# Gates of the middle group added by indirect transfers into cleared arrays, in place of one-hot products

## The chip, the cores and the metric

The kernel runs on one core of a Trainium2 chip. The metric is the device time of one execution in microseconds; the number compared is the median of three runs. Engines are named as in the profile: PE (TensorE), DVE (VectorE), ACT (ScalarE), POOL (GpSimd) and SP (SyncE, which issues most transfers).

## What is computed

One decoder layer over 1024 tokens of width 1024: a mixer (latent attention and retention, merged by gates) and then a channel mixer of single-neuron experts. The change touches the second:

```python
q = (x @ w_peer_q).reshape(T, 8, 128)            # 8 heads
s1, s2 = q[..., :64] . keys_1, q[..., 64:] . keys_2   # 128 keys each
v1, i1 = top_k(s1, 16); v2, i2 = top_k(s2, 16)
sc, ci = top_k(v1[:, None] + v2[None, :], 16)    # 16 pairs per head
eidx = e1 * 128 + e2                             # one of 16384 experts
gates = softmax(sc)                              # 8 x 16 gates per token
act = gelu(x . peer_u[eidx])
y = sum_k gates_k * act_k * peer_v[eidx_k]
```

So each token has 128 (expert, gate) pairs, and the same expert may come from two heads, whose gates add.

## The kernel before

The 1024 tokens are 8 blocks of 128, in three groups: blocks 0 to 2, 3 and 4, 5 to 7 (`GROUPS`, line 29). For each group the mixer runs in order: `latents` (projections to queries and keys), `mix` (retention and attention, interleaved), `merge`, `output` (projection, norm, top-k scores). `interleave` (line 284) weaves two generators by the counts in `STEPS`. The weights come in pieces of 512 KB through a ring of three `raw` tiles; each piece is split by ACT into a high part `whi` and by DVE into a rest `wlo` (`split_piece`, line 220), and every product is three matmuls (`mm3`).

Side work runs from two queues, `background[0]` and `background[1]`. `pace` (line 165) gives each queue a credit for each weight piece, by the rates in `RATES`; a queue's generators run while they have credit, each step costing what it yields. So how many side steps run is set by pieces, not by time.

The experts are done in two ways. For blocks 0 to 2 the rows of `peer_u` and `peer_v` are gathered: `gathered` (line 1059, in `background[1]`) fetches one row per token with an indirect transfer from POOL (line 1064, 512 KB), four rows ahead, and DVE takes one dot product (line 1081) or one weighted addition (line 1090) per step; 256 steps a block, 1.2 of credit each. For blocks 3 to 7 all 16384 experts are computed densely, in `dense` (line 1130). There a key e is one value of e2, with 128 experts: `scores(e)` (line 1152) multiplies one piece of `peer_u` with the 640 tokens. The first 48 keys (`AHEAD`) are computed in a first stage and stored in `gl_d`; then, in the last stage, groups of 8 keys are multiplied by their gates (`weights`, line 1213) and with `peer_v`, summed in PSUM, and added to y.

The gates of the dense blocks form a matrix of 128 x 128 experts by tokens. `gate_matrix` (line 1097) makes it from one-hot products: for 8 tokens DVE compares the two key indices with a ramp (line 1120), ACT copies one result, DVE multiplies the other by the gates (line 1123), PE multiplies the two for each token (line 1108), ACT copies the product out (line 1110), and after 32 tokens SP stores 2 MB to `gate_d` (line 1113). That is 16 steps per block, 80 in all, run from `background[0]` during the first dense stage. In the last stage `gate_tile` (line 1202) loads the gates of four keys in rows of 512 bytes.

For blocks 3 and 4 the pairs are chosen (`choose`, line 982) while the last group's mixer runs; what comes out is kept in `routed` until the dense stage. The start of `dense` loads these blocks' tokens back from `xT_d` (line 1144).

Of the kernel before, what the change touches and what calls it, by code (L numbers as in the profile page):

```python
# [12 lines left out]
F32 = mybir.dt.float32  # L13
# [10 lines left out]
P = 128  # L24
# [4 lines left out]
GROUPS = ((0, 1, 2), (3, 4), (5, 6, 7))  # L29
NGROUP = 1  # L30
NGATH = sum(len(g) for g in GROUPS[:NGROUP])
ND = NBLK - NGATH
# [15 lines left out]
DELAY = 8.0  # L48
STEPS = (((86, 72), (116, 64), (116, 144)), ((112, 90), (112, 90), (112,)), (80, 50))
HEAD = 20  # L50
# [44 lines left out]
def layout(inputs):  # L95
# [34 lines left out]
    col = lambda v: np.ascontiguousarray(v.reshape(-1, P).T)  # L130
    o["g_cols"] = np.concatenate([col(a["g_ret_gn"][0]), col(a["g_q_lora"][0]), col(a["g_kv_lora"][0])], 1)
    o["g_mix"] = a["g_mix"]
# [12 lines left out]
def hybrid_layer(ctx: ExitStack, tc: tile.TileContext, out, a, dbg=None):  # L145
# [48 lines left out]
    def bcast(ap, n, off=0):  # L194
# [8 lines left out]
            for g, blocks in enumerate(GROUPS[NGROUP:-1])]  # L203
    gate_d = dram.tile([DT // TS, P, P * TS], F32, name="gate_d")
    gl_d = dram.tile([AHEAD, P, DT], F32, name="gl_d")
# [98 lines left out]
    routed = []  # L304
    routing = []


# [7 lines left out]
    def group(g):  # L315
# [273 lines left out]
        def retention(hp):  # L589
# [5 lines left out]
            if meta:  # L595
                nc.sync.dma_start(tab[:, nbk], tb[:, NBLK])
            qk = rp.tile([P, nb, 4, 2, 32], F32, name="qk")
            tb2 = rp.tile([P, nb, 4, 2, 32], F32, name="yn")
# [191 lines left out]
        def open_mix():  # L790
            finish(0, LEAVE[0][g])
            own.mps, mp = pool("mp")
            own.oT = [mp.tile([P, W], F32, name=f"oT{k}") for k in range(4)]
            own.yT = [mp.tile([P, W], F32, name=f"yT{k}") for k in range(KD)]
            own.rps, own.rp = pool("rp")
            own.qb = own.rp.tile([P, nbk, 2, P], F32, name="qbd")
            V.memset(own.qb, 0.0)
            own.retentions = chain(*(retention(hp) for hp in range(4)))

        def mix():  # L800
            start(1)
            aps, own.ap = pool("ap")
            interleave([own.retentions, attention()], STEPS[0][g])
            aps.close()
            own.rps.close()

# [39 lines left out]
        def output():  # L846
# [20 lines left out]
            if not last:  # L867
                if g >= NGROUP:
                    ktp = ctx.enter_context(tc.tile_pool(name=f"kt{g}", bufs=1, side="right", reuse_waits="tile"))
                fcs, fc = pool("fc", "right")  # L870
                scs = [pool(f"sc{i}_", "right") for i in reversed(range(nbk))][::-1]
            xps, xp = pool("xp", "right")
            xT = [xp.tile([P, KD, W], F32R, name=n) for n in ("xT_hi", "xT_lo")]
# [57 lines left out]
            def route_pairs(i):  # L931
                found = yield from choose(blocks[i], *top[i], fc, ktp)
                if ktp:
                    routed.append(found)
                else:
                    background[1].append(gathered(blocks[i], *found))
# [45 lines left out]
    def choose(b, tv, ti, fp, ktp=None):  # L982
# [61 lines left out]
        if not ktp:  # L1044
            eidx = work.tile([P, 128], I32, name="eidx", bufs=NGATH)
            V.scalar_tensor_tensor(eidx, e12[:, 0], 128.0, e12[:, 1], op0=OP.mult, op1=OP.add)
            return eidx, gate
        pt = zacc()[:, 0]
        for s in range(2):
# [9 lines left out]
    def gathered(b, eidx, gate):  # L1059
# [16 lines left out]
        for n in range(256):  # L1076
# [5 lines left out]
            else:  # L1082
# [14 lines left out]
    def gate_matrix(i, kt, gT, iota_2, p):  # L1097

        stage = {}

        def products(t8, pairs):
# [10 lines left out]
            if t8 == t0 + TS - 8:  # L1112
                nc.sync.dma_start(gate_d[(P * i + t0) // TS], stage[0].rearrange("p e t -> p (e t)"))

        pending = None
        for t8 in range(0, P, 8):
            at = lambda t: t.rearrange("p (q r) -> p q r", r=2).unsqueeze(2).to_broadcast([P, 4, P, 2])
            eq = [p.tile([P, 4, P, 2], BF16, name=f"eq{n}", bufs=2) for n in range(2)]
            for n in range(2):
                V.tensor_tensor(eq[n], iota_2.unsqueeze(1).to_broadcast([P, 4, P, 2]), at(kt[:, n, t8:t8 + 8]), OP.is_equal)  # L1120
            pairs = [p.tile([P, 4, P, 2], F32, name=n, bufs=2) for n in ("oa", "ob")]
# [8 lines left out]
    def dense(xT):  # L1130
        nt = DT // TS
        pacing["rates"] = RATES[3]
        last = GROUPS[-1]
        segments = [(xT, len(last) * P)]
        xdp = ctx.enter_context(tc.tile_pool(name="xd", bufs=1, side="right", reuse_waits="tile"))
        for g, blocks in enumerate(GROUPS[NGROUP:-1]):
            w = P * len(blocks)
            t = [xdp.tile([P, KD, w], F32R, name=f"x_{n}{g}") for n in ("hi", "lo")]
            per = 1024 // w
            for dst, src in zip(t, xT_d[g]):  # L1140
                for j in range(0, KD, per):
                    n = min(per, KD - j)
                    raw = wp.tile([P, 1024], F32, name="raw", bufs=RING)
                    nc.sync.dma_start(raw[:, :n * w].rearrange("p (j c) -> p j c", j=n), src[:, j:j + n])
                    S.activation(dst[:, j:j + n].rearrange("p j c -> p (j c)"), raw[:, :n * w], AF.Copy)
            segments.insert(g, (t, w))
# [3 lines left out]
        up = ups.enter_context(tc.tile_pool(name="up", bufs=1, reuse_waits="tile"))  # L1150

        def scores(e):
# [11 lines left out]
        def routes():  # L1164
# [16 lines left out]
            for i, (kt, gT) in enumerate(routed):  # L1181
                yield from gate_matrix(i, kt, gT, iota_2, gm)
            gms.close()
# [16 lines left out]
        gts = deque()  # L1200
# [25 lines left out]


        es = [4 * n + k for n in sorted(range(P // 4), key=lambda n: (n + 0.5) / AHEAD if 4 * n < AHEAD else
                                        (n + 0.5 - AHEAD / 4) / (P - AHEAD)) for k in range(4)]
        gate_tile(es[0])  # L1230
        for e0 in range(0, P, GE):
# [35 lines left out]
    ident = load_const("ident", a["c_ident"], [P, P])  # L1267
    g_cols = load_const("g_cols", a["g_cols"], [P, 13])
    g_gn, g_ql, g_kvl = g_cols[:, 0:8], g_cols[:, 8:11], g_cols[:, 11:13]
    g_gnh = const.tile([P, 8], F32, name="g_gnh")  # L1270
# [58 lines left out]
```

## Time and profile before

| | us |
|---|---|
| median of three runs | 3496.61 (3493.37 to 3500.15) |
| profiled execution | 3493.31 |
| its span, first to last instruction | 3491.5 |
| TensorE busy (matmul) | 3291.3 (94%) |
| VectorE busy | 2611.3 (75%) |
| ScalarE busy | 1261.8 (36%) |
| GpSimd busy | 1159.7 (33%) |
| mean busy share of the 16 DMA engines, 837 MB | 240 GB/s |

The stages, by the first and last instructions of their lines: group 0 to about 540 us, group 1 to 980, group 2 to 1420, first dense stage to 1955, last stage to 3490. A busy share over the whole span mixes these; for a change in one stage the rows of that stage count. Matmuls overlap in the pipeline, so durations of single ones add to more than the busy time.

### The profile page before, as it was taken

What the parts mean: (1) busy time and instruction counts of PE and PEld (TensorE: products, weight loads), DVE (VectorE), ACT (ScalarE), POOL (GpSimd) and SP (SyncE); (2) the same over time, 40 slices, a digit from 0 to 9 for tenths busy, and PEclk for the clock granted to TensorE, in tenths of its full rate; (3) what the DMA queues carried; (4) which work ended last, traced back from release to release, by engine and by line L of the source; (5) the groups of instructions that cost most, each with busy time, mean ns of one, the idle gap of its engine ahead of it and who ended that gap; (6) DMA issues with size and microseconds to landing.
All of it is one profiled execution on the core that took longest, in us unless ns stands there. A gap on an engine that the chain in (4) does not pass through costs nothing.

```text
span 3491.5 us, 53120 instructions
## 1 busy us (share of the span) xinstructions
PE 3291.3 (94%) x20376; PEld 3003.2 (86%) x20376; DVE 2611.3 (75%) x5118; ACT 1261.8 (36%) x2097; POOL 1159.7 (33%) x821
## 2 busy tenths in 40 slices
PE   8899989989789999899999899999999999999999
PEld 7788988788767799799999887888898888888888
DVE  4434458987697577689898687888888878878885
ACT  3445344544345533324666322222222222222221
POOL 0100000122211122012454354554556545555452
PEclk9999999999899999899999999999999999999999
DMA  3422354456744458446877998988989898989895
GB/s 132 124 78 85 123 188 135 151 179 235 255 148 142 136 200 297 160 156 209 309 285 286 338 314 285 326 317 310 321 305 345 300 328 309 334 304 318 308 333 182
DMA packets 329247, 837.10 MB, mean 240 GB/s; under 512 B 45712, under 2 KB 140688, under 8 KB 326176
## 3 DMA queue, kind: packets, MB, share of 16 engines
q1 hardware_dynamic: 218400, 431.00, 35.9%
q0 software_dynamic: 110592, 402.70, 32.8%
q8 instruction: 160, 2.62, 0.3%
q14 instruction: 95, 0.78, 0.1%
HBM read 755.16 MB, written 78.43 MB: 239 GB/s over the span
## 4 chain that ended last, share of the span: by engine, by line
PE 36%; issue 24%; POOL 11%; DVE 8%; DMA 5%; ACT 2%; POOLq 0%; SPq 0%; DVEq 0%; ACTq 0%
POOL row L1064 10%; PE zacc L245 7%; PE zacc L247 7%; PE zacc L246 7%; PE tr L245 3%; PE tr L246 3%; PE tr L247 3%; DMA row<-in_peer_v_dram,eidx 2%; PE tr L764 2%; DVE wlo L218 2%; DMA gl<-gl_d 1%; PE sc L728 1%; DVE row L1081 1%; PE sc L774 1%; DVE top_i L975 1%
## 5 line engine op out<-in xcount | busy, mean ns | idle before, releaser
L217 ACT ACTIVATE whi<-raw 128x1024 fp32r<-128x1024 f32 (+2 forms) x508 | 520.5, 1026 | 1337.5 <-PE zacc L247 619.7
L218 DVE TENSOR_TENSOR wlo<-raw,whi 128x1024 fp32r<-128x1024 f32 (+2 forms) x508 | 600.1, 1183 | 434.0 <-ACT whi L217 433.1
L1064 POOL DMA_INDIRECT row<-in_peer_u_dram,eidx x384 | 490.2, 1277 | 1004.1 <-DVE row L1081 791.3
L1064 POOL DMA_INDIRECT row<-in_peer_v_dram,eidx x384 | 602.7, 1570 | 610.8 <-DVE acc L1090 259.4
L245 PE MATMUL zacc<-whi,c_hi 128*128 128x512 f32 x1280 | 506.4, 396 | 39.1 <-DVE y L1254 37.6
L247 PE MATMUL zacc<-whi,c_lo 128*128 128x512 f32 x1280 | 504.5, 394 | 5.1 <-DVE c_lo L218 5.1
L246 PE MATMUL zacc<-wlo,c_hi 128*128 128x512 f32 x1280 | 504.1, 394 | 0.0
L1081 DVE SCALAR_TENSOR_TENSOR row<-row,xn 128x1024 f32<-128x1024 f32 x384 | 462.5, 1221 | 37.5 <-DMA row<-in_peer_u_dram,eidx 26.4
L245 PE MATMUL tr<-xT_hi,whi 128*128 128x384 f32 (+1 forms) x1216 | 410.8, 338 | 17.3 <-ACT gl L1161 16.2
L246 PE MATMUL tr<-xT_lo,whi 128*128 128x384 f32 (+1 forms) x1216 | 407.9, 335 | 0.0
L247 PE MATMUL tr<-xT_hi,wlo 128*128 128x384 f32 (+1 forms) x1216 | 407.5, 335 | 0.0
L245 PEld LDWEIGHTS zacc<-whi,c_hi 128*128 128x128 f32 x1280 | 244.3, 191 | 94.1 <-issue 36.4
L245 PE MATMUL tr<-x_hi,whi 128*128 128x256 f32 x1024 | 294.1, 287 | 9.6 <-ACT whi L217 9.6
L247 PEld LDWEIGHTS zacc<-whi,c_lo 128*128 128x128 f32 x1280 | 244.0, 191 | 58.9 <-DVE c_lo L218 7.2
L246 PE MATMUL tr<-x_lo,whi 128*128 128x256 f32 x1024 | 288.7, 282 | 0.0
L247 PE MATMUL tr<-x_hi,wlo 128*128 128x256 f32 x1024 | 288.6, 282 | 0.0
L246 PEld LDWEIGHTS zacc<-wlo,c_hi 128*128 128x128 f32 x1280 | 244.5, 191 | 50.3
L1090 DVE SCALAR_TENSOR_TENSOR acc<-row,dots,acc 128x1024 f32<-128x1024 f32 x192 | 246.0, 1281 | 18.3 <-DMA row<-in_peer_v_dram,eidx 17.8
L245 PE MATMUL zacc<-whi,hn_hi 128*128 128x256 f32 x832 | 250.7, 301 | 1.8 <-ACT pT L779 1.3
L1090 DVE SCALAR_TENSOR_TENSOR xn<-row,dots,xn 128x1024 f32<-128x1024 f32 x189 | 241.9, 1280 | 9.1 <-DMA row<-in_peer_v_dram,eidx 8.9
L245 PEld LDWEIGHTS tr<-xT_hi,whi 128*128 128x128 f32 x1216 | 231.3, 190 | 19.0 <-ACT gl L1161 16.8
L246 PE MATMUL zacc<-wlo,hn_hi 128*128 128x256 f32 x832 | 238.3, 286 | 0.9 <-DVE wlo L218 0.9
(268 smaller groups left out, 6929.5 us busy)
## 6 DMA issues: line engine op xcount, KB each, us to landing
raw<-in_peer_ut_dram SPq DMA_DIRECT2D x128, 512.0 KB, 5.4
raw<-in_peer_vt_dram SPq DMA_DIRECT2D x128, 512.0 KB, 6.6
gate_d<-stage SPq DMA_DIRECT2D x20, 2048.0 KB, 8.4
gt<-gate_d SPq DMA_DIRECT2D x32, 1280.0 KB, 9.8
raw<-in_w_nat_dram SPq DMA_DIRECT2D x72, 512.0 KB, 3.5
raw<-in_w_z_dram SPq DMA_DIRECT2D x48, 512.0 KB, 3.7
gl_d<-gl SPq DMA_DIRECT2D x48, 320.0 KB, 4.4
gl<-gl_d SPq DMA_DIRECT2D x48, 320.0 KB, 8.0
```

Of the source, the lines that this page charges most:

```text
L217: S.activation(hi, src, AF.Copy)
L218: V.tensor_tensor(lo, src, hi.bitcast(F32), OP.subtract)
L245: T.matmul(o, st[0], mv[0], start=first, stop=False)
L246: T.matmul(o, st[0], mv[1], start=False, stop=False)
L247: T.matmul(o, st[1], mv[0], start=False, stop=last)
L728: T.matmul(sc[:, c, 0:w], qh, kT[0:96, k0:k0 + w], start=True, stop=c < nch - 1)
L764: T.matmul(oo, vh[:, c + k], pT[:, k], start=False, stop=c + k == b)
L774: T.transpose(pt[:, P * k:P * k + P], pr[:, k0:k0 + P], ident)
L975: V.max_index(ti[:, 0:8], tv[:, 0:8], src)
L1064: G.indirect_dma_start(out=row, out_offset=None, in_=table, in_offset=bass.IndirectOffsetOnAxis(ap=eidx[:, k:k + 1], axis=0))
L1081: op = V.scalar_tensor_tensor(row, row, 1.0, xn, op0=OP.mult, op1=OP.mult, accum_out=dots[:, k:k + 1])
L1090: op = V.scalar_tensor_tensor(acc[k % 2], row, dots[:, k:k + 1], acc[k % 2], op0=OP.mult, op1=OP.add)
```

## The change

The gates of blocks 3 and 4 are no longer made by `gate_matrix`. Two arrays `gate_s` in memory, of 8 MB each, are cleared by 64 transfers from a tile of zeros, queued in `background[0]` in group 0. `choose` returns for these blocks an index per (token, pair) into the array, and the gate. `scattered` issues 128 indirect transfers per block from POOL, each adding one value per token; each step of `gathered` runs one step of each block that is ready. What is left runs after the first dense stage. `gate_d` holds only the last group's gates and is laid out by fours of keys, so that a gate tile is one transfer of 6 KB rows and two of 2 KB rows from `gate_s`. The first gate tile takes the last group's part from the stage by an ACT copy. The y tiles are loaded after the first group's weights. The stored tokens are loaded in `output` of the last group. For groups 1 and 2 the attention pool is opened before the retention pool; the block matrix `qbd` is cleared in the first retention step; one interleaving count goes from 90 to 100. The comparisons of `gate_matrix` are kept in program order.

```diff
+NSCAT = len(GROUPS[1]) * P // 32
-STEPS = (((86, 72), (116, 64), (116, 144)), ((112, 90), (112, 90), (112,)), (80, 50))
+STEPS = (((86, 72), (116, 64), (116, 144)), ((112, 90), (112, 100), (112,)), (80, 50))
...
+    place = (t // TS * 4 * TS + t % TS).astype(np.float32)
...
-    gate_d = dram.tile([DT // TS, P, P * TS], F32, name="gate_d")
+    gate_d = dram.tile([P // 4, P, DT // TS - NSCAT, 4 * TS], F32, name="gate_d")
+    gate_s = [dram.tile([P * P * P, 1], F32, name=f"gate_s{b}") for b in GROUPS[1]]
...
+            if not hp:
+                V.memset(qb, 0.0)
...
+            own.aps = None
+            if g:
+                own.aps, own.ap = pool("ap")
             own.rps, own.rp = pool("rp")
             own.qb = own.rp.tile([P, nbk, 2, P], F32, name="qbd")
-            V.memset(own.qb, 0.0)
...
+            if last:
+                segments.extend(stored_tokens())
             xps, xp = pool("xp", "right")
...
                 if ktp:
-                    routed.append(found)
+                    spread.append(scattered(gate_s[i], *found))
                 else:
                     background[1].append(gathered(blocks[i], *found))
...
+        if b in GROUPS[1]:
+            sh = fp.tile([P, 128], I32, name="sh")
+            V.tensor_copy(sh, e12[:, 1])
+            V.tensor_scalar(sh, sh, 2, None, op0=OP.logical_shift_right)
+            at = fp.tile([P, 128], F32, name="pf")
+            V.scalar_tensor_tensor(at, e12[:, 0], 16.0, e12[:, 1], op0=OP.mult, op1=OP.add)
+            V.tensor_scalar(at, at, 4.0 * 8, place, op0=OP.mult, op1=OP.add)
+            sidx = ktp.tile([P, 128], I32, name=f"sidx{b}")
+            V.scalar_tensor_tensor(sidx, sh, float(P * 4 * P - P), at, op0=OP.mult, op1=OP.add)
+            sg = ktp.tile([P, 128], F32, name=f"sg{b}")
+            V.tensor_copy(sg, gate)
+            return sidx, sg
...
             tc.keep_in_program_order(op)
+            for steps in spread:
+                next(steps, None)
             yield 1.2
...
+    def cleared():
+        for t in gate_s:
+            view = t.rearrange("(q p h c) o -> p q h (c o)", p=P, h=2, c=256)
+            for q in range(0, P // 4, 2):
+                for k in range(2):
+                    nc.sync.dma_start(view[:, q:q + 2, k], zeros.unsqueeze(1).to_broadcast([P, 2, 256]))
+                yield 2.0
+
+    def scattered(dst, sidx, gate):
+        for k in range(128):
+            G.indirect_dma_start(out=dst, out_offset=bass.IndirectOffsetOnAxis(ap=sidx[:, k:k + 1], axis=0),
+                                 in_=gate[:, k:k + 1], in_offset=None, compute_op=OP.add)
+            yield
...
             if t8 == t0 + TS - 8:
-                nc.sync.dma_start(gate_d[(P * i + t0) // TS], stage[0].rearrange("p e t -> p (e t)"))
+                n, (e, gt) = (P * i + t0) // TS, first
+                nc.sync.dma_start(gate_d[:, :, n].rearrange("q p c -> p q c"), stage[0].rearrange("p (q e) t -> p q (e t)", e=4))
+                S.activation(gt[:, NSCAT + n], stage[0][:, e:e + 4], AF.Copy)
...
         finish(0)
         pacing["rates"] = RATES[5]
+        for steps in spread:
+            for _ in steps:
+                pass
...
             ys.append(vp.tile([P, D], F32, name=f"y{b}"))
-            nc.sync.dma_start(ys[-1], h2_d[b])
...
         def gate_tile(e):
-            gts.append(vp.tile([P, nt, 4, TS], F32, name="gt", bufs=GTB))
-            nc.sync.dma_start(gts[-1], gate_d[:, :, TS * e:TS * e + 4 * TS].rearrange("n p (e t) -> p n e t", e=4))
+            gts.append(gtp.tile([P, nt, 4, TS], F32, name="gt", bufs=GTB))
+            nc.sync.dma_start(gts[-1][:, NSCAT:].rearrange("p n e t -> p n (e t)"), gate_d[e // 4])
+            scattered_gates(e)
+
+        def scattered_gates(e):
+            per = P // TS
+            for i, t in enumerate(gate_s):
+                nc.sync.dma_start(gts[-1][:, per * i:per * i + per].rearrange("p n e t -> p (n e t)"),
+                                  t.rearrange("(q p c) o -> q p (c o)", p=P, c=4 * P)[e // 4])
+
+        scattered_gates(es[0])
...
+            if not e0:
+                for b, y in zip(range(NGATH, NBLK), ys):
+                    nc.sync.dma_start(y, h2_d[b])
...
+    zeros = const.tile([P, 256], F32, name="zeros")
+    V.memset(zeros, 0.0)
+    background[0].append(cleared())
```

## Rows read from the trace of the kernel before

**Rows 1.** The page, part 1: busy time, share, instructions by engine.
```profile
PE 3291.3 (94%) x20376; PEld 3003.2 (86%) x20376; DVE 2611.3 (75%) x5118; ACT 1261.8 (36%) x2097; POOL 1159.7 (33%) x821
```

**Rows 2.** Stages: window, length, busy per engine (count), PE clock, DMA share, GB/s.
```profile
152.00:460.00 308.00, 292.26 (x1977) 264.37 (x1978) 133.15 (x307) 137.85 (x315) 12.51 (x11) 0.99 0.32 104
1243.00:1397.00 154.00, 154.00 (x984) 153.84 (x983) 109.16 (x176) 52.21 (x76) 44.07 (x39) 1.00 0.77 264
1628.00:1940.00 312.00, 311.80 (x2372) 311.21 (x2373) 282.32 (x315) 196.13 (x228) 151.63 (x59) 1.00 0.78 287
1940.00:1990.00 50.00, 35.48 (x244) 35.28 (x243) 21.98 (x18) 8.03 (x14) 19.13 (x16) 0.90 1.03 387
1990.00:3450.00 1460.00, 1414.72 (x7500) 1260.48 (x7501) 1187.35 (x1431) 358.45 (x494) 763.12 (x557) 0.98 0.90 314
```

**Rows 3.** Gate products: line 1108 in its window (PE, PEld); comparisons, count, min/median/max ns.
```profile
1628.00:1940.00 312.00, 160.44 (x1280) 155.87 (x1280) 1.00 0.78 287
...
L1120 DVE TENSOR_TENSOR eq<-iota,kt x160: 676/686/716, 1407.2 to 1928.3; 128x1024 bf16<-128x1024 bf16 x160
```

**Rows 4.** ACT's timeline, start and duration: two score keys, no gate step between.
```profile
1944.51 1.06 ACT L217 ACTIVATE whi<-raw 128x1024 fp32r<-128x1024 f32 x1 [3.61 <-PE tr L246]
...
1951.51 1.06 ACT L217 ACTIVATE whi<-raw 128x1024 fp32r<-128x1024 f32 x1 [3.60 <-PE tr L246]
```

**Rows 5.** When blocks 3 and 4 are routed; gather issues by window (POOL busy, count).
```profile
1036.99 0.36 ACT L1053 ACTIVATE kt<-zacc 128x256 bf16<-128x256 f32 x1
...
1114.55 0.38 ACT L1053 ACTIVATE kt<-zacc 128x256 bf16<-128x256 f32 x1 [0.78 <-PE zacc L1051]
...
1037.00:1115.00 78.00, 11.88 (x11) 1.00 0.49 154
1115.00:1243.00 128.00, 16.53 (x15) 1.00 0.40 128
1243.00:1397.00 154.00, 42.72 (x38) 1.00 0.77 264
1397.00:1628.00 231.00, 28.33 (x22) 0.95 0.49 167
1628.00:1955.00 327.00, 158.57 (x65) 1.00 0.79 291
```

**Rows 6.** Indirect issues, a run of comparisons; landing in 1240:1400; 4 KB loads, 1000:1240.
```profile
632.62 0.94 POOL L1064 DMA_INDIRECT row<-in_peer_u_dram,eidx  x1 [0.30 <-issue]
...
1723.77 5.03 POOL L1064 DMA_INDIRECT row<-in_peer_v_dram,eidx  x1 [0.30 <-issue]
...
1725.51 2.49 DVE L1120 TENSOR_TENSOR eq<-iota,kt 128x1024 bf16<-128x1024 bf16 x4
...
DMA to landing us min/median/max: 4.1/6.5/8.6
...
vh<-v_d SPq DMA_DIRECT2D x6, 4.0 KB, 3.2
```

**Rows 7.** Hand-over: SP's timeline, and PE's waits in 1950:2000 (total, times, longest).
```profile
1959.98 19.11 SPq L1190 DMA_DIRECT2D gl_d<-gl  x1
...
PE tr L245 <- ACT gl L1161: 15.7, 1, 15.7
```

**Rows 8.** PE's waits in 1400:1440, the start of the dense stage.
```profile
PE tr L245 <- ACT whi L217: 9.6, 1, 9.6
```

**Rows 9.** Timeline at the start of the last group's mixing.
```profile
988.00 2.95 PE L728 MATMUL sc<-kT,qT 96*128 96x392 f32 x4 [9.94 <-DMA qT<-qT_d]
```

**Rows 10.** DMA queues in 2000:3440 (packets, MB, share), gate tiles; PE's longest wait there.
```profile
q0 software_dynamic: 79548, 289.66, 55.8%
q1 hardware_dynamic: 113856, 163.07, 33.7%
...
gt<-gate_d SPq DMA_DIRECT2D x30, 1280.0 KB, 10.0
...
PE zacc L245 <- DVE y L1254: 37.6, 11, 6.7
```

More of the change, by code (lines that the diff above doesn't have):

```diff
@@ L130, in layout @@
     col = lambda v: np.ascontiguousarray(v.reshape(-1, P).T)
-    o["g_cols"] = np.concatenate([col(a["g_ret_gn"][0]), col(a["g_q_lora"][0]), col(a["g_kv_lora"][0])], 1)
+    t = np.arange(P)
+    place = (t // TS * 4 * TS + t % TS).astype(np.float32)
+    o["g_cols"] = np.concatenate([col(a["g_ret_gn"][0]), col(a["g_q_lora"][0]), col(a["g_kv_lora"][0]),
+                                  place[:, None]], 1)
     o["g_mix"] = a["g_mix"]
@@ L305, in hybrid_layer @@
     routing = []
+    spread = []
     def open_pool(name, side="left"):
@@ L801, in mix @@
             start(1)
-            aps, own.ap = pool("ap")
+            if not g:
+                own.aps, own.ap = pool("ap")
             interleave([own.retentions, attention()], STEPS[0][g])
-            aps.close()
-            own.rps.close()
+            for pools in (own.rps, own.aps) if g else (own.aps, own.rps):
+                pools.close()
         def open_merge(following):
@@ L1094, in gathered, with stored_tokens, gate_matrix @@
         nc.sync.dma_start(out[P * b:P * b + P], acc[0])
-    def gate_matrix(i, kt, gT, iota_2, p):
+    segments = []
+    def stored_tokens():
+        xdp = ctx.enter_context(tc.tile_pool(name="xd", bufs=1, side="right", reuse_waits="tile"))
+        for g, blocks in enumerate(GROUPS[NGROUP:-1]):
+            w = P * len(blocks)
+            t = [xdp.tile([P, KD, w], F32R, name=f"x_{n}{g}") for n in ("hi", "lo")]
+            per = 1024 // w
+            for dst, src in zip(t, xT_d[g]):
+                for j in range(0, KD, per):
+                    n = min(per, KD - j)
+                    raw = wp.tile([P, 1024], F32, name="raw", bufs=RING)
+                    nc.sync.dma_start(raw[:, :n * w].rearrange("p (j c) -> p j c", j=n), src[:, j:j + n])
+                    S.activation(dst[:, j:j + n].rearrange("p j c -> p (j c)"), raw[:, :n * w], AF.Copy)
+            yield t, w
+    def cleared():
[10 more added lines that the diff above has]
+            yield
+    def gate_matrix(i, kt, gT, iota_2, p, first):
         stage = {}
@@ L1119, in gate_matrix @@
             for n in range(2):
-                V.tensor_tensor(eq[n], iota_2.unsqueeze(1).to_broadcast([P, 4, P, 2]), at(kt[:, n, t8:t8 + 8]), OP.is_equal)
+                tc.keep_in_program_order(V.tensor_tensor(
+                    eq[n], iota_2.unsqueeze(1).to_broadcast([P, 4, P, 2]), at(kt[:, n, t8:t8 + 8]), OP.is_equal))
             pairs = [p.tile([P, 4, P, 2], F32, name=n, bufs=2) for n in ("oa", "ob")]
@@ L1133, in dense @@
         last = GROUPS[-1]
[L1134 to L1146, printed above, removed]
+        segments.append((xT, len(last) * P))
         starts = [sum(w for _, w in segments[:k]) for k in range(len(segments))]
@@ L1150, in dense @@
         up = ups.enter_context(tc.tile_pool(name="up", bufs=1, reuse_waits="tile"))
+        gtp = ups.enter_context(tc.tile_pool(name="gtp", bufs=1, reuse_waits="tile"))
+        es = [4 * n + k for n in sorted(range(P // 4), key=lambda n: (n + 0.5) / AHEAD if 4 * n < AHEAD else
+                                        (n + 0.5 - AHEAD / 4) / (P - AHEAD)) for k in range(4)]
+        gts = deque([gtp.tile([P, nt, 4, TS], F32, name="gt", bufs=GTB)])
         def scores(e):
@@ L1181, in routes @@
             for i, (kt, gT) in enumerate(routed):
-                yield from gate_matrix(i, kt, gT, iota_2, gm)
+                yield from gate_matrix(i, kt, gT, iota_2, gm, (es[0], gts[0]))
             gms.close()
@@ L1198, in dense @@
             ys.append(vp.tile([P, D], F32, name=f"y{b}"))
-            nc.sync.dma_start(ys[-1], h2_d[b])
-        gts = deque()
         def gate_tile(e):
-            gts.append(vp.tile([P, nt, 4, TS], F32, name="gt", bufs=GTB))
-            nc.sync.dma_start(gts[-1], gate_d[:, :, TS * e:TS * e + 4 * TS].rearrange("n p (e t) -> p n e t", e=4))
+            gts.append(gtp.tile([P, nt, 4, TS], F32, name="gt", bufs=GTB))
[7 more added lines that the diff above has]
+        scattered_gates(es[0])
         def activations(e):
@@ L1225, in weights @@
             return hi, lo
-        es = [4 * n + k for n in sorted(range(P // 4), key=lambda n: (n + 0.5) / AHEAD if 4 * n < AHEAD else
-                                        (n + 0.5 - AHEAD / 4) / (P - AHEAD)) for k in range(4)]
-        gate_tile(es[0])
         for e0 in range(0, P, GE):
@@ L1267, in hybrid_layer @@
     ident = load_const("ident", a["c_ident"], [P, P])
-    g_cols = load_const("g_cols", a["g_cols"], [P, 13])
-    g_gn, g_ql, g_kvl = g_cols[:, 0:8], g_cols[:, 8:11], g_cols[:, 11:13]
+    g_cols = load_const("g_cols", a["g_cols"], [P, 14])
+    g_gn, g_ql, g_kvl, place = g_cols[:, 0:8], g_cols[:, 8:11], g_cols[:, 11:13], g_cols[:, 13:14]
+    zeros = const.tile([P, 256], F32, name="zeros")
+    V.memset(zeros, 0.0)
+    background[0].append(cleared())
     g_gnh = const.tile([P, 8], F32, name="g_gnh")
```

## The prediction

> **What bounds the kernel now.** I read the page's first two parts, then a table of stages, then the waits inside each stage. TensorE is busy for 94% of the span [rows 1]. The stages differ. In the merge and projection of the last group (1243 to 1397 us) and in the stretch that builds the gates (1628 to 1940 us) it is busy without a gap: 154.0 of 154 us and 311.8 of 312 us [rows 2]. What leaves PE there shortens the kernel, as long as nothing else is late. From 1940 to 1990 us PE is busy only 35 of 50 us, at a granted clock of 0.90, with the DMA engines full at 1.03 [rows 2]. In the last stage (1990 to 3450) PE is busy 1414.7 of 1460 us at clock 0.98, and the DMA engines are at 0.90 [rows 2]: nearly two limits at once. POOL is idle for most of the span, but its queue is in order, and this change puts its new work there.
>
> **The change part by part.** All sums are against the profiled execution, 3493.3 us (span 3491.5), which lies 3.3 us under the median of 3496.6.
>
> *Gate products of two blocks go.* The matmuls of line 1108 hold PE for 160.4 us of the gate stretch [rows 3], in 80 steps of 8 tokens: 2.0 us a step. Blocks 3 and 4 are 32 of these steps: 32 x 2.0 = 64 us, on the path because PE has no gap there. DVE loses two comparisons of 0.686 us and a product per step [rows 3]; DVE and ACT are beside PE, so that adds nothing. Is PE free to use the time? A score key takes 7.0 us alone [rows 4]; a key earns 6.5 x 0.9 = 5.85 units for the routes and a gate step costs 1.7, so 3.44 steps go with one key, 7.0 + 6.9 = 13.9 us. With 48 steps instead of 80 the products fill 14 keys instead of 23, and the last 13 or so of the 48 stored keys run at 7.0 us. Value -64.
>
> *Index arithmetic, copies.* Per block, five small DVE operations come and three transposes and two ACT copies go; 12 ACT copies of a piece of the stage into the first gate tile come. ACT is at 196 of 312 us in that stretch [rows 2], under PE's cover. Value 0; without cover about 5 us.
>
> *Stored tokens loaded before the output projection instead of at the start of the expert stage.* At that start PE waits 9.6 us for the first whi piece [rows 8], whose load stands behind these four loads in SP's queue and behind the ring of raw tiles. They now run under the projection's matmuls. Next late are the normalised rows and their transposes, which stay. Value -8, ends 0 and -16 (the wait gone, and PE back at full clock sooner).
>
> *The hand-over from stored keys to the products.* Five y loads and a gate tile of 2560 packets are issued here; the next store then holds SP for 19.1 us, and PE waits 15.7 us [rows 7]. The y loads now come after the first group's weights, where the first use is dozens of microseconds off, and the first gate tile is partly copied on chip. Its two scattered parts wait for all scatters, with the raw loads behind them on SP. Value -16, ends 0 and -22 (with the clock).
>
> *Attention pool opened first, qbd cleared later.* At the start of the last group's mixing PE waits 9.9 us for qT [rows 9]. Tiles move in memory, so their loads may be let go earlier. A gain is not sure, since SP's order also has raw loads ahead. Value -6, ends +3 and -16. The count 100 for 90 in one interleaving shifts latents against merge; 0, ends -6 and +6.
>
> *Gate tiles laid out by fours of keys.* The gathers' 289.66 MB are 70.7 thousand packets of 4 KB in 55.8% of 1440 us x 16 engines: 0.18 us each. The hardware queue's 33.7% are 7764 us; 30 gate tiles of 2560 packets are 39 of its 163 MB, the other 124 MB cost 5450 us at that price, and 2314 us stay for 76800 packets of 512 bytes: 30 ns each [rows 10]. A gate tile costs the 16 engines 2560 x 30 / 16 = 4.8 us now; as rows of 6 KB and 2 KB it is 3.6 us. That is 38 us less over 32 tiles, the share falling from 0.90 to about 0.87. PE's one large wait there is for the y additions, 37.6 us [rows 10], which a DMA reaches only through DVE's rows. Value -5, ends 0 and -40. The stores turn into 4096 packets, 7.7 us each instead of 5.8 by the same prices, but 12 instead of 20: value 0, ends 0 and +12.
>
> *Clearing.* 64 DMAs of 256 KB, 16.8 MB: at 0.18 us per 4 KB 46 us of all engines, in a stage at 0.32 [rows 2]. SP issues them between piece loads. Value +4, ends 0 and +20 (what is left is issued in one run at the merge, ahead of raw loads).
>
> *Scatters.* 256 indirect DMAs of 128 single values, two per gather step, each adding into an array that the one before also writes. Two additions into one tensor depend on each other, and the program orders dependent transfers by waits, so I expect POOL to wait for each landing, with the next gather and POOL's small powers (norms, retention) behind it, and DVE's row operation, in order, behind the gather. The first block's indices are there at 1037 us, the second's at 1115 [rows 5]. From then on the gather steps are 11, 15, 38, 22 and 65 to 1955 us [rows 5]; the pacing is by pieces, not time, so these counts stay. The scatters end 23 and 12 steps before the stored keys do, and the drain behind them is empty. How long is a step? One issue is 0.94 + 0.30 us when nothing blocks it [rows 6]: three make 3.7. A step lasts 154 / 38 = 4.05 us in the merge, 13.9 / 2.44 = 5.7 in the gate stretch (34 steps; a key earns 6.5 x 0.45 / 1.2 = 2.44 gather steps), and 7.0 / 2.44 = 2.9 in the pure score stretch, where 19 steps still carry a scatter. So the period P from one scatter to the next decides. No scatter is in the trace. Bounds: 3.2 us, the landing of a 4 KB transfer; 6.5 us, the median landing of a gather, whose fastest is 4.1 [rows 6]. I take 4.4: the scatter runs behind a gather in the same queue but moves 512 bytes. Merge: 38 x 0.35 = 13, of which the rows fetched four steps ahead cover 9. Gate stretch: 0. Pure scores: 19 x 1.5 = 28, less 5. Waiting norms: 4. Value +32 (rounded), ends 0 and +177.
>
> *A rule against this change.* In the gate stretch a gather issue takes 158.6 / 65 = 2.4 us on the mean, and single ones 5.03 us where DVE runs through comparisons and a product without a break [rows 5, 6]. The Trainium skill, "SBUF — State Buffer", section "Who interferes with whom", says that a VectorE instruction with two SBUF inputs blocks a GpSimd instruction that reads SBUF until it ends. The 5.03 us agrees with it. By that rule the result is the third rival below.
>
> Sum: -64 - 8 - 16 - 6 - 5 + 4 + 32 = -63: 3430 us, on the median's footing 3434.
>
> **The rivals.**
> *Scatters hidden.* If a scatter lands in under 3 us, P is set by the issues, and the four rows ahead cover the rest. For it: the 3.2 us of the small transfer. Against it: the DMA engines are at 0.77 in the merge [rows 2], and gathers need 4.1 at least. With the stalls at -10, -19 and -10 and the tiles at -16: -64 - 55 = -119, 3378 us. "DMA: Bandwidth & Descriptors" of the Trainium skill, section "Anatomy of one DMA — SWDGE (gpsimd) path", gives such a DMA about 2.0 us fixed, which speaks for this case; no run here shows one so small. For a gather an estimate by its formula (2.0 us + bytes / 436 GB/s) is 3.2 us; the trace has 6.5 [rows 6], so there the page does not hold under this load.
>
> *The scatter chain becomes the bound.* If a scatter lands only with the gather ahead of it, P is 6.5. Merge: 38 x 2.45 = 93; gate stretch: 34 x 0.8 = 27; scores: 19 x 3.6 = 68; less 15 of lead, plus 4: +177 against gains of 95 net of the clearing: +82, 3579 us. Below 5.7 us the cost is 38 (P - 4.05) + 19 (P - 2.9) - 11 = 57 P - 220; it passes the gains of 95 at P of about 5.5 us, and from there the kernel is slower. For it: the same software queue, in order, with 512 KB ahead of each pair. Against it: the gather's own bytes are most of its 6.5 us.
>
> *POOL is locked out by DVE in the gate stretch.* With 2.4 + 0.3 us for each of three issues a step takes 8.2 us instead of 5.7: 34 x 2.5 = 85 us, on top of the 32: -95 + 117 = +22, 3519 us. Against it: other issues beside the same comparisons are short, and the change keeps the comparisons in program order, which breaks up runs of four such as the 2.49 us one [rows 6].
>
> *The freed PE time is not used* because gathers at 2.44 rows in 7.0 us starve DVE: about 3490 us.
>
> **How the numbers follow.** Forecast 0.50 (3395 to 3475), hidden 0.22, chain 0.15, lock-out 0.10, not used 0.03. A measurement of this kernel tells about 0.2%, 7 us. Faster: the forecast and the hidden case but for their edges, 0.71; same 0.06; slower 0.23. For 8 in 10 the range takes the forecast, the hidden case and the lock-out and leaves out the chain: 3370 to 3525.
>
> **What would show it.** Line 1108 at 48 steps and about 96 us; score keys 7.0 us apart behind them. POOL's scatters with their own waits: the distance between two of one block in the merge gives P; if PE has gaps there, with DVE waiting for rows, the chain case holds. The PE wait of 15.7 us gone. Packets of 512 bytes gone from the last stage, DMA share at 0.87. Wrong altogether it would be if the scatters were not done before the stored keys: then SP stands at the first gate tile, and PE with it.

## The result, and the profile after

The changed kernel takes 3656.61 us (median of 4 runs, 3655.32 to 3658.56) against 3494.99 for the kernel before in the same comparison: a ratio of 1.0458, 95% interval 1.0441 to 1.0475. The forecast was 3434, with a range of 3370 to 3525. The page of after, first busy times, then the group of the scatters, answers to [rows 1]:

```profile
PE 3271.4 (90%) x19858; PEld 2970.8 (81%) x19858; DVE 2537.0 (69%) x5035; ACT 1203.4 (33%) x2041; POOL 1558.6 (43%) x1077
...
L1152 POOL DMA_INDIRECT gate_s<-sg,sidx x256 | 434.3, 1697 | 191.4 <-DMA gate_s<-sg,sidx 138.8
```

TensorE has less work than before and is idle far longer. Where, a table of stages says. Columns: window, length, busy time of PE, PEld, DVE, ACT and POOL with counts, granted clock, DMA share, GB/s ([rows 2] for before):

```profile
1100.00:1243.00 143.00, 99.30 (x658) 79.22 (x656) 54.31 (x130) 50.76 (x109) 106.10 (x69) 0.85 0.45 97
1243.00:1397.00 154.00, 104.39 (x636) 96.62 (x637) 63.51 (x115) 42.33 (x80) 125.57 (x78) 0.81 0.49 107
1397.00:1650.00 253.00, 131.87 (x702) 126.13 (x700) 83.99 (x126) 44.57 (x60) 192.54 (x127) 0.75 0.57 144
...
1900.00:2060.00 160.00, 160.00 (x1214) 159.53 (x1213) 150.76 (x169) 103.61 (x127) 59.27 (x32) 1.00 0.93 308
...
2170.00:3620.00 1450.00, 1414.98 (x7547) 1260.96 (x7546) 1191.66 (x1435) 358.89 (x495) 777.96 (x557) 0.99 0.88 317
```

From 1100 to 1650 us PE is busy 335.6 of 550 us. The granted clock is 0.75 to 0.85 there, between TensorE's two levels (1.2 and 2.4 GHz), for 1.00 from 1243 to 1397 us before [rows 2]. The gate stretch (1900 to 2060) has no gap, and the last stage is as full as it was. A tile view of two landmarks cuts each kernel in three: the first copy of a gate stage (the gate stretch begins) and the last store of a stored key (the hand-over). First the kernel before, then after. Columns: duration min/median/max in ns, first and last start in us.

```profile
L1110 ACT ACTIVATE stage<-zacc x80: 1024/1025/1033, 1630.6 to 1938.0; 128x1024 f32<-128x1024 f32 x80
...
L1190 SPq DMA_DIRECT2D gl_d<-gl x48: 319/320/19114, 1437.1 to 1991.1; - x48
```

```profile
L1169 ACT ACTIVATE stage<-zacc x48: 1017/1025/1035, 1885.9 to 2066.7; 128x1024 f32<-128x1024 f32 x48
...
L1245 SPq DMA_DIRECT2D gl_d<-gl x48: 319/320/5081, 1668.0 to 2170.4; - x48
```

Up to the gate stretch the kernel lost 255.3 us (1885.9 for 1630.6). From there to the hand-over it gained 76.0 (284.5 for 360.5), and 16.6 in the last stage (1483.8 for 1500.4 to the end of the span). So the gains came and the loss is in one place: the stretch in which the scatters run. Issues on POOL there, the scatters (line 1152) first, then the gathers (line 1089), with POOL's busy time, count, granted clock, DMA share, GB/s; last, the sums of after's merge on DVE (durations in ns, first and last start in us):

```profile
1020.00:1243.00 223.00, 122.22 (x71) 0.89 0.47 110
1243.00:1397.00 154.00, 105.26 (x61) 0.81 0.49 107
...
1020.00:1243.00 223.00, 26.08 (x22) 0.89 0.47 110
1243.00:1397.00 154.00, 17.53 (x15) 0.81 0.49 107
...
L852 DVE SCALAR_TENSOR_TENSOR mg<-zt,zacc x8: 545/548/549, 1349.8 to 1528.7; 128x384 f32<-128x384 f32 x8
```

From 1243 to 1397 us, which was the merge before, there are 61 scatters to 15 gathers, not two to one, and before there were 38 gathers in the same time [rows 5]. (After is late by then and still mixing: its merge's sums start at 1350 us.) The framework's planner decides the order on POOL's queue: only the row operations on DVE are held in the order of the program, so scatters, ready early, were put ahead of gathers and small powers. POOL's timeline (start, duration, what ended the idle time before) shows what one costs:

```profile
1422.19 1.09 POOL L1089 DMA_INDIRECT row<-in_peer_u_dram,eidx  x1 [0.30 <-issue]
1423.59 1.57 POOL L1152 DMA_INDIRECT gate_s<-sg,sidx  x1 [0.30 <-issue]
1425.47 1.55 POOL L1152 DMA_INDIRECT gate_s<-sg,sidx  x1 [0.31 <-issue]
...
1433.48 2.31 POOL L1152 DMA_INDIRECT gate_s<-sg,sidx  x1 [0.95 <-DMA gate_s<-sg,sidx]
```

An issue is 1.55 us and 0.30 behind it, against 0.94 and 0.30 for a gather of a thousand times the bytes [rows 6]. From 1020 to 1755 us, where the last scatter starts, POOL is busy 524 us, and it stood idle just before scatters for 191 us more, 139 of them waits for a landing: 716 of 735 us. DVE's waits in 1020 to 1900 us (total, times, longest), then those on POOL's powers in 1020 to 2180 us of the kernel before, where DVE had no wait for the rows of a dot product, then PE's in after:

```profile
DVE row L1106 <- DMA row<-in_peer_u_dram,eidx: 189.6, 36, 18.8
DVE nm_gn L675 <- POOL rs_gn L218: 71.5, 4, 34.2
...
DVE xnt L914 <- POOL r_f L218: 34.7, 2, 24.0
```

```profile
DVE nm_gn L667 <- POOL rs_gn L213: 4.4, 3, 1.8
...
DVE xnt L901 <- POOL r_f L213: 1.3, 2, 0.7
```

```profile
PE zacc L252 <- DVE wlo L223: 48.8, 12, 10.8
PE sc L736 <- ACT yn L678: 47.4, 2, 34.2
PE tr L277 <- DVE xnt L914: 33.9, 2, 19.8
```

The chain can be read off: gathers and norms stand behind scatters on POOL; DVE, in order, stands at the row or the norm; the weight pieces that DVE splits for PE come late.

### The profile page after: what moved, and what is told of

It reads as the page before. It is cut to its first block, busy times and chain, and to the rows that moved or that the text cites. A ratio compares the mean times of both kernels' runs of the same rounds, so it can differ in the third digit from the quotient of the medians.

```text
span 3654.2 us, 52338 instructions
## 1 busy us (share of the span) xinstructions
PE 3271.4 (90%) x19858; PEld 2970.8 (81%) x19858; DVE 2537.0 (69%) x5035; ACT 1203.4 (33%) x2041; POOL 1558.6 (43%) x1077
## 4 chain that ended last, share of the span: by engine, by line
PE 31%; issue 20%; POOL 16%; DMA 11%; DVE 8%; ACT 1%; POOLq 0%; SPq 0%; DVEq 0%; ACTq 0%
POOL row L1089 9%; DMA gate_s<-sg,sidx 6%; PE zacc L250 6%; POOL gate_s L1152 6%; PE zacc L252 6%; PE zacc L251 6%; PE tr L250 3%; PE tr L251 3%; PE tr L252 3%; DMA row<-in_peer_v_dram,eidx 2%; DVE wlo L223 1%; DMA gl<-gl_d 1%; PE tr L772 1%; DVE row L1106 1%; DMA xn<-xn_d 1%
## 5 line engine op out<-in xcount | busy, mean ns | idle before, releaser
L1089 POOL DMA_INDIRECT row<-in_peer_v_dram,eidx x384 | 552.5, 1439 | 580.2 <-DVE acc L1115 231.0
L1089 POOL DMA_INDIRECT row<-in_peer_u_dram,eidx x384 | 507.4, 1321 | 652.5 <-DVE row L1106 472.7
L1152 POOL DMA_INDIRECT gate_s<-sg,sidx x256 | 434.3, 1697 | 191.4 <-DMA gate_s<-sg,sidx 138.8
```

What stands on the lines that cost most here:

```text
L1089: G.indirect_dma_start(out=row, out_offset=None, in_=table, in_offset=bass.IndirectOffsetOnAxis(ap=eidx[:, k:k + 1], axis=0))
L1152: G.indirect_dma_start(out=dst, out_offset=bass.IndirectOffsetOnAxis(ap=sidx[:, k:k + 1], axis=0), in_=gate[:, k:k + 1], in_offset=None, c ...
```

## The experiments

Three theories. A: the scatters' place and issue time on POOL's queue. B: each scatter's wait for the landing of the one before into the same array. C: another part of the change. The times below are medians, in us, with the 95% interval of the ratio to the kernel before; the three spans come from the profiled run, cut at the landmarks above. The kernel before was timed beside each, with medians of 3490.7 to 3495.7, so a difference between two rows is good to about 10 us unless they were timed together.

| kernel | time | ratio | to the gate stretch | to the hand-over | to the end |
|---|---|---|---|---|---|
| before | 3495.0 | | 1630.6 | 360.5 | 1500.4 |
| after | 3656.6 | 1.0441 to 1.0475 | 1885.9 | 284.5 | 1483.8 |
| e1 no scatters | 3387.9 | 0.9664 to 0.9723 | 1620.5 | 284.4 | 1478.6 |
| e5 products for all | 3469.9 | 0.9897 to 0.9950 | 1615.9 | 344.3 | 1507.9 |
| e4 four arrays | 3713.3 | 1.0592 to 1.0655 | 1943.9 | 286.1 | 1481.2 |
| e2 in order | 3577.4 | 1.0184 to 1.0263 | 1712.2 | 375.0 | 1487.7 |
| e6 in order, four arrays | 3514.4 | 1.0047 to 1.0090 | 1701.3 | 333.9 | 1483.0 |
| e3 in order, plain | 3506.7 | 1.0037 to 1.0074 | 1671.8 | 342.3 | 1483.4 |
| e11 in order, plain, four | 3461.0 | 0.9868 to 0.9931 | 1678.2 | 292.5 | 1495.8 |
| e8 one block | 3592.2 | 1.0269 to 1.0325 | 1783.2 | 316.0 | 1488.5 |
| e9 one block, in order | 3496.4 | 0.9996 to 1.0030 | 1657.0 | 343.1 | 1493.2 |
| e10 and two arrays | 3500.4 | 1.0004 to 1.0031 | 1627.4 | 316.8 | 1557.0 |
| e12 and summed by DVE | 3436.8 | 0.9819 to 0.9870 | 1626.7 | 319.3 | 1488.7 |

**Is it the scatters?** The first leaves them out; the other keeps products for all five blocks and the rest of the change, without the clearing.

```diff
 # e1, in scattered()
-            G.indirect_dma_start(out=dst, ..., compute_op=OP.add)
 # e5
-NSCAT = len(GROUPS[1]) * P // 32
+NSCAT = 0
...
-                    spread.append(scattered(gate_s[i], *found))
+                    routed.append(found)
... (the clearing, the index arithmetic and the loads of gate_s go too)
```

> The changed kernel without the 256 indirect transfers of single values (the gates of blocks 3 and 4 stay zero); everything else of the change stays, the clearing, the index arithmetic, the layout by fours and the loads of the cleared arrays too. If the transfers on POOL's queue cause the loss, whether by their place in it (theory A) or by waiting for each other's landing (theory B): 3385 to 3410 us, the forecast's sum without its term for them. If another part of the change causes it, such as the clearing or the order of the pools (theory C): above 3550.

> The kernel before with the other parts of the change: gates of all five blocks by products, but laid out by fours of keys, the first gate tile partly copied on the chip, stored tokens and y loaded at their new places, the pools reordered, 100 for 90. No clearing, no scatters. By the prediction's terms -8 - 16 - 6 - 5 = -35 us against before: 3460 (3440 to 3475). If these parts gain nothing of their own, 3490 to 3500.

3387.9 and 3469.9: both as expected. Theory C falls; the scatters cost 3656.6 - 3387.9 = 268.7 us, and the table puts 265 of them before the gate stretch. The rest of the change, without scatters and with products for all, is worth 0.8% by itself. The chain on POOL is gone in e1: DVE waits 2.0 us for rows between 1020 and 2180 us, for 189.6 in after. The clock has a part in the loss, too. PE's busy time in e1:

```profile
PE 3227.6 (95%) x19858; PEld 2938.1 (87%) x19858; DVE 2535.1 (75%) x5035; ACT 1202.0 (36%) x2041; POOL 1107.6 (33%) x821
```

For the same 19858 matmuls after is busy 3271.4 us, 43.8 more, at a mean granted clock of 0.95 for 0.983. So about 44 of the 269 us are PE's own work, run at a lower clock, and the rest is idle time.

**Order, or landing?** e2 holds gathers and scatters in program order; e4 leaves the order to the planner and takes the landing waits away.

```diff
 # e2, gathers and scatters alike
-            G.indirect_dma_start(out=dst, ...)
+            tc.keep_in_program_order(G.indirect_dma_start(out=dst, ...))
 # e4
-            G.indirect_dma_start(out=dst, ...)
+            G.indirect_dma_start(out=dst[k % 4], ...)
```

> The changed kernel with each indirect transfer of POOL, the single values and the gathers, held in the order in which the program writes them: two scatters to a gather step, none ahead of its step. Theory A (what costs is that scatters stand ahead of gathers and norms in POOL's queue): a step then takes 2 x 1.86 + 1.24 = 5.0 us of POOL and the time falls to 3430 to 3500. Theory B (the wait of each scatter for the landing of the one before into the same array): the waits stay, so above 3600.

> The changed kernel with the scatters of a block dealt in turn to four arrays, so that none waits for the landing of the one before it; three of the four arrays are neither cleared nor read, which leaves three quarters of these gates out of the result. The place of the scatters in POOL's queue is left to the planner as before. Theory A: the issues alone fill the queue ahead of the gathers, 1.86 us each, so the loss shrinks by the 139 us of waits at most and not below 3550. Theory B: 3400 to 3450.

e4 without waits is 57 us slower than after, not faster: theory B falls as the cause of the whole. Line 1153 issues the scatters here, line 1090 the gathers; columns as above, and then the start of the merge's sums:

```profile
1243.00:1397.00 154.00, 120.37 (x76) 0.74 0.38 58
...
1243.00:1397.00 154.00, 8.34 (x8) 0.74 0.38 58
```

```profile
L853 DVE SCALAR_TENSOR_TENSOR mg<-zt,zacc x8: 544/548/549, 1578.9 to 1678.6; 128x384 f32<-128x384 f32 x8
```

The scatters run as one burst, 76 of them to 8 gathers in these 154 us, and the merge comes only behind it. But e4 changed two things. Free of the dependences, the planner put the scatters still further ahead: POOL's timeline has 30 gathers ahead of the last of 256 scatters (counted from 1015 us), for 73 in after. So e4 doesn't tell what the waits alone cost; e6, with the order held, does. e2 gains 79 us, so the order is a cause, but it hit neither expectation: 190 us over e1 remain. The same two counts in 1243 to 1397 us, mostly its merge, line 1152 and line 1089:

```profile
1243.00:1397.00 154.00, 85.25 (x52) 0.92 0.64 170
...
1243.00:1397.00 154.00, 31.85 (x26) 0.92 0.64 170
```

Now two to one, and a step lasts 154 / 26 = 5.9 us where the work beside it takes 154 / 38 = 4.05 [rows 5]. The order alone doesn't make POOL fast enough.

**What makes the step long?** In program order, without landing waits (e6), with plain writes in place of additions (e3), and with both (e11).

```diff
 # e6
-            ...indirect_dma_start(out=dst, ...)
+            ...indirect_dma_start(out=dst[k % 4], ...)
 # e3
-            ...in_=gate[:, k:k + 1], in_offset=None, compute_op=OP.add))
+            ...in_=gate[:, k:k + 1], in_offset=None))
 # e11: both edits
```

> The order of the program kept on POOL, and each block's scatters dealt to four arrays of which one is read (three quarters of these gates are left out of the result). It takes the 83 us of landing waits out of the kernel with the program's order (3577 us). If what is left of its loss, 190 us against the kernel without scatters (3388), is the time of the issues on POOL, the step shrinks from 5.9 to about 2 x 1.9 + 1.3 = 5.1 us and the time is 3490 to 3560. If it is the landing waits: 3400 to 3450.

> The kernel with the program's order, its scatters writing instead of adding (a pair that two heads choose keeps one of its gates, so some sums are left out of the result). If it is the addition that makes a scatter's issue 1.55 us against a gather's 0.94, the issues fall by 256 x 0.6 = 154 us of POOL and the time goes to 3420 to 3480. If it is the scatter of single values itself: the issue stays at 1.55 us and the time within 15 us of 3577.

> Both blocks scattered in the program's order, with plain writes (issue 0.98 us) and four arrays to a block (no landing waits); the result holds a quarter of these gates. If the length of POOL's step against the work beside it is the whole of the cost, a step of 3 x 1.28 = 3.8 us lies under the merge's 4.05 and the gate stretch's 5.7, and only the pure score stretch (2.9) pays: 3390 to 3425, near the 3388 without scatters. If the scatters cost by something else than POOL's time (their packets on the DMA engines, the landing of gathers behind them): above 3450.

e6 saves 63 us, which is the price of the landing waits at this order (3514 lies in the range for the issues as the larger part). e3 saves 71 and missed both its ranges: the addition is what makes an issue long, but with shorter issues the landing waits grew, from 83.0 us in e2 to 126.1. Both edits together save 116. The tile view of e3 shows the price of the addition: 0.986 us for a plain issue in the median, 1.57 for an adding one in e2.

```profile
L1152 POOL DMA_INDIRECT gate_s<-sg,sidx x256: 965/986/4972, 1025.1 to 1956.7; - x128
...
L1152 POOL DMA_INDIRECT gate_s<-sg,sidx x256: 1542/1570/6737, 1026.9 to 2028.4; - x128
```

e11 missed the range for POOL's step and came out in its other branch, above 3450: it is 73 us over e1. The step was not 3.8 us. In the merge an issue took 1.18 us in the mean (110.75 us for 94), not 0.98, and 31 gathers started from 1259.6 to 1392.7 us, 4.4 us apart, where the work beside them takes 4.05. DVE waits for rows 53.2 us in 26 pieces between 1020 and 2020 us:

```profile
1243.00:1397.00 154.00, 141.49 (x831) 136.26 (x830) 95.68 (x155) 51.15 (x80) 110.75 (x94) 0.99 0.67 211
...
DVE row L1107 <- DMA row<-in_peer_u_dram,eidx: 53.2, 26, 4.5
...
1258.02 1.35 POOL L219 TENSOR_TENSOR rs_gn<-v_gn,mhalf 128x6 f32<-128x6 f32 x1 [22.16 <-DVE v_gn L673]
```

That branch named packets on the DMA engines and later landings, and the trace shows neither: the engines' share in these 154 us is 0.67, for 0.81 in e1, and where DVE waited it had the row 5.1 us after its issue in the median (24 rows), for a median landing of 6.0 us in e1. The rows are asked for late: a gather is issued 16 us in the median after DVE let its buffer go, for 0.3 us in e1. The queue falls behind when POOL stands 22.2 us at a norm's power with the gathers behind it (the last line), and with a step longer than the merge's it doesn't catch up. e12, below, stands 28.6 us at the same place and then issues a gather every 3.9 us: there DVE waits 30.4 us for rows (1020 to 2000 us). So a queue that is nearly full isn't hidden work: it has nothing left to make up a delay with. How the 73 us divide was not taken apart by a run.

**One block only.** Block 4 goes back to products, so there is one scatter to a step; once in the planner's order, once in the program's.

```diff
+SCAT = GROUPS[1][:1]
...
-        if b in GROUPS[1]:
+        if b in SCAT:
 # e9 also: keep_in_program_order on gathers and scatters
```

> Only block 3 scattered, as above, with the place of the scatters left to the planner. Theory A: they stand ahead of gathers and norms again from 1020 us on, 128 of them at 3.2 us from landing to landing, and half of the 269 us is lost: 3388 + 41 + 134 = 3563 (3500 to 3600). If the loss is by POOL's total load alone, no worse than in order: 3425 to 3450.

> Only block 3 scattered, block 4 by products with the last group; the program's order kept on POOL, so one scatter to a gather step. If POOL's queue is the bound only where its steps are longer than the work beside them: a step of 1.24 + 2.4 = 3.7 us stays under the merge's 4.05, so the scatters are nearly hidden, and half of the 82 us of products is saved against the kernel by products (3470): 3425 to 3450. If the cost goes with the number of scatters: 3388 + 41 + 95 = 3524 (3500 to 3545).

e8 is 3592.2, as theory A said, and e9, with the same work, 3496.4: the order alone is 96 us. But e9 is neither hidden (3425 to 3450) nor clearly in proportion (3500 to 3545). POOL's timeline in its merge shows a wait that the expectation had left out:

```profile
1326.18 1.58 POOL L1155 DMA_INDIRECT gate_s<-sg,sidx  x1 [2.25 <-DMA gate_s<-sg,sidx]
1328.07 0.99 POOL L1092 DMA_INDIRECT row<-in_peer_u_dram,eidx  x1 [0.30 <-issue]
1330.74 1.58 POOL L1155 DMA_INDIRECT gate_s<-sg,sidx  x1 [1.69 <-DMA gate_s<-sg,sidx]
1332.63 0.98 POOL L1092 DMA_INDIRECT row<-in_peer_u_dram,eidx  x1 [0.30 <-issue]
```

With one array, each scatter waits for the landing of the last: 32 in 154 us, 4.8 a step. These waits are 50.4 of the 154 us, for 9.0 in the same window of after: here theory B is the bound, though it wasn't there.

**One block, no waits.** Even and odd pairs go to two arrays. e10 adds the second array to the gate tile by a transfer on POOL's queue; e12 loads it on SP and adds on DVE.

```diff
 # both, on e9
-            ...indirect_dma_start(out=dst, ...)
+            ...indirect_dma_start(out=dst[k % 2], ...)
 # e10, with the gate tile
+            second.append(lambda: G.dma_start(part, src[1], accum_op=OP.add))
 # e12, with the gate tile (GLB = 3 for its memory)
+            nc.sync.dma_start(second[-1], src[1])
 # e12, before the tile's first use
+            V.tensor_tensor(part, part, second.popleft(), OP.add)
```

> Only block 3 scattered, in the program's order, adding, but even and odd pairs into two arrays, of which the second is added to the gate tile by a transfer from POOL's queue (32 of them in the last stage). The step then has no landing wait: 1.9 + 1.3 = 3.2 us against 4.8 with one array. If the landing wait is what one block in order (3496 us) still lost: gate stretch begun by about 1630, its end 20 us sooner, 3435 to 3455, under the kernel by products (3470). If the adding transfers hold POOL's gathers up in the last stage, or the waits were not the cause: 3470 to 3500.

> As the kernel with one block scattered into two arrays in the program's order, but the second array's part is loaded by SP into a tile of its own and added to the gate tile by VectorE (32 additions of 128 x 512); for its memory one of the four gl buffers goes. The adding transfers on POOL's queue, which waited 178 us for gate tiles in the last stage, are gone. If they were what lost the 70 us of the last stage: 1944 us to the last stored key, as there, and a last stage of 1485 to 1510: 3430 to 3460, under the kernel by products (3470). If the last stage stays near 1557 us, something else of the second array costs it, its loads or the missing buffer: 3490 to 3510.

Up to the hand-over both did as expected: the gate stretch begins at 1627 us, within 7 of the kernel without scatters, and 1944 and 1946 at the last stored key. e10 lost all of it in the last stage, so that its 3500.4 us lie at the edge of its second branch. POOL's waits there, 1950 to 3490 us:

```profile
POOL row L1092 <- DVE row L1109: 189.6, 114, 10.8
POOL gt L1272 <- DMA gt<-gate_s: 177.9, 12, 30.2
```

The adding transfer waits for the tile's load, up to 30 us, with the gathers behind it: the same mistake once more, a waiting instruction on the queue that feeds DVE. e12 takes it off POOL: 3436.8 us, 0.9845 of before, as expected, and under e5 with intervals that don't meet. Its tile view and its merge:

```profile
L1172 ACT ACTIVATE stage<-zacc x64: 1016/1025/1030, 1626.7 to 1873.3; 128x1024 f32<-128x1024 f32 x64
...
1243.00:1397.00 154.00, 148.76 (x918) 147.61 (x917) 109.42 (x167) 59.76 (x90) 126.46 (x79) 0.99 0.88 275
```

POOL is as busy as in the same window of after (126 of 154 us), but gathers and scatters stand in the order of their use, four waits for a landing are 5.1 us in all, and PE is back at 148.8.

## Why the prediction was wrong, point by point

The spans below are differences of single profiled runs, and times of the kernel before spread over 25 us (3479.75 to 3505.27), so a term of a few us is borne out by its wait rather than by its span.

- *Gate products*: -64 predicted. e5 and e1 differ by these (and the scattered blocks' arrays): 344.3 to 284.4, -59.9. Right.
- *Stored tokens and the attention pool*: -8 and -6. The gate stretch begins 14.7 us sooner in e5 than before. The wait of 9.6 us [rows 8] is gone there, and the one of 9.9 for qT [rows 9] is 5.4: 14.1 together. Right in sum.
- *Hand-over*: -16. Gate stretch to last store is 344.3 in e5 for 360.5 with the same products, -16.2. In place of the wait of 15.7 us [rows 7] e5 has 4.7, and in after PE's largest from 2100 to 2300 us is 3.2. Right.
- *Clearing*: +4. e1, with it, begins the gate stretch 4.6 us later than e5, which is in range but not clear of the spread. The clearing ran from 14 us on and not in the stage at 0.32 that the prediction took; the DMA share of the first 150 us rose from 0.38 to 0.73, and PE's busy time in them stayed at 129 us.
- *Gate tiles by fours*: -5, not confirmed as one number. The last stage is 7.5 us longer in e5 than before and 21.8 shorter in e1. PE's wait for y [rows 10] is 39.9 us in all in e5 and 18.6 in e1. Packets of 512 bytes are gone from the last stage of both (in e5 they have moved to the stores), and the DMA share fell from 0.90 to 0.88 in after; what shortens the stage in e1 and after alone is open.
- *Sum of all but the scatters*: -95 predicted, 3387.9 - 3495.7 = -107.8 measured; most of the difference is the last stage of e1.
- *Scatters*: +32 predicted, +268.7 measured. This is the step that failed, in three of its parts, and by a term that it lacked.
  - "Two per gather step": I read the program's loop as the order of the queue. The prediction names POOL's in-order queue but takes the loop's order for granted; the planner lifted the scatters. That costs 79 us (after to e2), and 96 with one block (e8 to e9).
  - "One issue is 0.94 + 0.30 us": the price of a gather taken for an addition of single values. It is 1.55 + 0.30. By this price alone two scatters and a gather are 4.9 us, above the 4.4 that I took for the whole period. Plain writes, 0.98, give back 71 us.
  - "So the period P decides", set by landing: the landing was guessed well (4.4; the median in e2's merge is 4.3, below), but it isn't the period. P in e2's merge is 5.9 us; by the prediction's own line 57 P - 220, with 34 x 0.2 for the gate stretch, that makes 123, and e2 lost 190 over e1. So the line was too low as well: it has nothing before the merge and next to nothing in the gate stretch, where a step was 6.9 us (42 scatters and 21 gathers in 1755 to 1900). Of e2's 190 us, 91 lie between the start of that stretch and the hand-over (375.0 for 284.4).
  - The clock has no term. After's matmuls took 44 us more than those of e1, and e2's 47 (3274.7 for 3227.6).

```profile
L1152 POOL DMA_INDIRECT gate_s<-sg,sidx x52: 1542/1568/2564, 1253.6 to 1396.3; - x52
...
DMA to landing us min/median/max: 2.9/4.3/6.8
```

Of the rivals, *the scatter chain becomes the bound* was nearest, with the right victim (gathers and norms on POOL, DVE behind them, PE behind DVE) and mostly the wrong agent: the order and the issue, with the landing waits for 63 us (e2 to e6). That its 3579 us is what the program's order gives (e2, 3577) is luck: landings of 6.5 us aren't there. *Locked out by DVE in the gate stretch* is not what cost: in after the last scatter starts at 1755 us, before the gate stretch. In e2, where 42 scatters did run beside the comparisons, one took 1.90 us in the mean (79.94 us) and not the 2.4 of that rival.

The Trainium skill, "DMA: Bandwidth & Descriptors", section "Anatomy of one DMA — SWDGE (gpsimd) path", calls descriptor generation small and puts most of the fixed cost into completion. Here the measurement decides otherwise: of 3.3 us from issue to landing (median in 1400 to 1650 us of after) the issue holds POOL for 1.55, about half. The section "Rules for kernel authors" of the same page of the Trainium skill wants the earlier transfer's semaphore waited for where an accumulating one touches the same bytes. The program does so, with 93 such waits of 138.8 us in after; what would be lost without them no run here shows. Two arrays are a way to have the waits end in time.

## What to carry to other kernels

Before a transfer is put on a queue that others share, write down the order in which the queue will really issue (a planner's order isn't the loop's), what each issue holds the queue, and who stands behind it; a queue that is busy for 43% of the span can be full for 700 us. Price an indirect transfer by its issue, not by its bytes, and one that adds above one that writes. Where dependent transfers wait for each other's landing, deal them to two arrays and add on an engine that has room.

## What the runs showed of the hardware

- An indirect transfer of 128 single values that adds takes 1.55 us to issue (median of after; 1.89 in e12 from 1243 to 1397 us), one that writes 0.98 (e3), a gather of 128 rows of 4 KB 0.94 to 1.01 where nothing holds it up.
- Adding scatters into one array follow each other at 3.2 us at best (POOL's timeline of after, 1102.57 to 1112.37 us: 3.2 to 3.4 apart) and at 4.8 with a gather between (e9).
- Clearing 16.8 MB in the first 120 us took the DMA share of the first 150 us from 0.38 to 0.73 and nothing from PE (129 us busy in both).
- A gather landed in 4.3 us (median) at a DMA share of 0.38 (e4, 1243 to 1397 us) and in 6.0 at 0.81 (e1, the same window).
- The same 19858 matmuls took 44 us more in after than in e1, with the granted clock at 0.75 to 0.85 while PE stood idle for two fifths of 1100 to 1650 us.
